# RWKV-7 inside a one-layer decoder trunk: chunk products kept per head in 64x64 blocks, the inverse joined once for all chunks, and chunk groups run offset with one projection k block per step

## The chip, the cores and the metric

The kernel runs on one core of a Trainium2 chip. The metric is the device time of one execution in microseconds (us), the median of several runs. A shorter time is better.

## What is computed

One layer of a hybrid decoder over 1024 tokens of width 1024, in fp32. A projection of the normed input feeds three mixers (HGRN-2, a dilated-window attention, RWKV-7); their outputs go through an output projection, and a gated feed-forward part and a per-layer embedding follow.

```python
z = rmsnorm(h) @ w_in                      # 1024 x 4096
o_a = hgrn2_mix(...); o_b = dilated_window_mix(...); o_c = rwkv7_mix(...)
h = h + concat(o_a, o_b, o_c) @ w_out
h = h + conv_glu_ffn(rmsnorm(h), ...)
h = h + sigmoid(rmsnorm(h) @ w_g) * (p @ w_p)
```

The change is in RWKV-7: four heads of 64, per head a 64x64 state that every token updates.

```python
def step(state, inp):                      # per head
    r_t, w_t, k_t, v_t, kk_t, a_t = inp
    sa = einsum('vk,k->v', state, -kk_t)
    state = state * w_t[None, :] + sa[:, None] * (kk_t * a_t)[None, :] + v_t[:, None] * k_t[None, :]
    return state, einsum('vk,k->v', state, r_t)
# then a group norm per head, a bonus (r k r_k) v, and a gate
```

## The kernel before

**Layout and precision.** Activations lie transposed, 128 rows of channels by 1024 tokens. A product with a weight is done in three matmuls on parts rounded to fp32r (`mm3`, L139, L141, L143: high x high, low x high, high x low). One projection of 128 output channels (tile `dp`, two PSUM banks, two buffers) is eight k blocks of six 128x512 matmuls, 48 in all. Its weight is loaded by SP (L107), rounded by ScalarE (`whi`, L116), and the remainder taken by GpSimd or VectorE (`wlo`, L118). Its result is scaled on VectorE and put through a sigmoid on ScalarE where it needs one (`zst`, L415 to L420), then stored to DRAM (`z`, L410) and loaded again by its user (`zl`, L448).

**RWKV in chunks.** A tile holds a pair of heads, 64 rows each; the head pairs are p = 0 and 1. The 1024 tokens are 16 chunks of 64. `rwkv_prep` makes the decayed operands `ar` (a and r), `bhat` and `khat`, `v` and the bonus (`bon`, L573). `rwkv_scores` (L608) makes all chunks' 64x64 scores in TensorE (`sc`), copied by ScalarE. `rwkv_inverse` inverts 32x32 blocks by substitution on VectorE for all chunks at once (L630, L632), and sends the two diagonal blocks through DRAM into the layout that the loop reads (`Tz`, `Uz` to `Tc`, L641; `T` on SP's queue, `U` on ScalarE's).

**The loop.** `rwkv_main` runs four groups of four chunks, one after the other (`rwkv_group`, L697 to L826). A group copies its operands into block-diagonal 128x128 tiles (`abd`, `bbd`, `kbd`, `addend`; GpSimd and ScalarE), transposes these and `v` (L732, L736), spreads the scores (L748) and the inverse's blocks (L756) over 128x128, joins the two halves of each inverse (`py` L763, `pu` L778, and a predicated copy), and then makes `pk`, `px` (L789), `pgm` (L796), `pn`, the chain of states (`pS`, with `S` on VectorE, L815) and the outputs `pyo`. `by_head` (L595) issues a product per head, 64x64; `px`, `pgm`, `py` and `pu` are 128x128 products on block-diagonal operands, half of them zeros. `rwkv_norm` normalises a half of the tokens and ends with output transposes (`yt`, L682) and the gate product (`pg`, L686).

**What sets the order.** The kernel is written under a tile framework whose scheduler orders every engine's instructions by when their parts were written and by dependences; a tile that takes over another tile's memory waits for that tile's last user. So the projections that the other mixers need (`project_rest`, 22 from a list `js`) serve as filler. `FILL` says how many are written where: six ahead of the first loop, four behind it, four ahead of the second and four behind it. Four go to the next phase. Behind each loop, the second half's `yt` and `pg` are written behind the third of the four projections (`finish` at i == 2), with the fourth after them. The scheduler moves a few matmuls of these projections into the loops and most into the preparation and the substitution.

**What follows.** HGRN and the attention run interleaved, with the four projections left (`zp`) as filler. The attention loads q, k, v of its first two heads on GpSimd's queue (L448), its mask on ScalarE's queue (L339), transposes v (`vt`, L1026) and makes scores (`swq`, L1043). HGRN's first loads are on SP's queue (L448).

Of the kernel before, what the change touches and what calls it, by code (L numbers as in the profile page):

```python
# [10 lines left out]
F32 = mybir.dt.float32  # L11
# [7 lines left out]
P = 128  # L19
# [18 lines left out]
CC_ID, CC_BONE, CC_MSK, CC_Q, CC_HG, CC_RU = 0, 128, 256, 512, 640, 640 + 9 * 128  # L38
NC0 = 640
NCC = CC_RU + 128  # L40


def shape_constants():
# [6 lines left out]
    c[:, CC_MSK:CC_MSK + P] = same & (pp < ff)  # L50
    c[:, CC_MSK + P:CC_MSK + 2 * P] = same & (pp <= ff)
# [5 lines left out]
    c[:, CC_Q:CC_Q + P] = pp // 32 == ff // 32  # L57
    c[:, CC_RU:CC_RU + P] = same & (ff % 64 >= 32) & (pp % 64 < 32)
# [33 lines left out]
class Trunk:  # L92
# [183 lines left out]
    def setup(self):  # L276
# [6 lines left out]
        self.msk = self.cst[:, CC_MSK:CC_MSK + 2 * P]  # L283
        self.qmask = self.cst[:, CC_Q:CC_Q + P]
        self.cmask = cp.tile([P, NCC - NC0], U8, name="cmask")
        self.umask = self.cmask[:, CC_RU - NC0:CC_RU - NC0 + P]
# [109 lines left out]
    def project_rest(self, js):  # L396
# [3 lines left out]
        for j in js:  # L400
            ps = self.proj(j)
# [9 lines left out]
            self.z[j] = d  # L411

# [49 lines left out]
    def rwkv(self):  # L462
# [7 lines left out]
        for p in (0, 1):  # L470
# [16 lines left out]

    def rwkv_prep(self, p, tp, lt, d):
# [57 lines left out]
        ar = self.slots.tile([P, 16, 2, 64], F32, tag="rk_ar", name=self.nm("ar"), bufs=1)  # L546
# [7 lines left out]
        nc.vector.scalar_tensor_tensor(ar[:, :, 0, 1:], kk3[:, :, 1:], -1.0, g3[:, :, :63], ALU.mult, ALU.mult)  # L554
        nc.scalar.activation(ar[:, :, 0, 0:1], kk3[:, :, 0:1], AF.Copy, scale=-1.0)
# [7 lines left out]
        nc.vector.tensor_tensor(ar[:, :, 1, :], c3(r), g3, ALU.mult)  # L563
# [13 lines left out]
    def block_diag(self, pool, name, src, eng):  # L577

        if (pool, name) not in self.bd:
            t = pool.tile([P, 4, 2, 64], F32, tag=name, name=self.nm(name), bufs=1)  # L580
            self.nc.gpsimd.memset(t, 0.0)
            self.bd[(pool, name)] = t
        t = self.bd[(pool, name)]
        for h in (0, 1):
# [27 lines left out]
    def rwkv_inverse(self, p, tp, d):  # L612
# [22 lines left out]
        for nm, t, q in (("T", Tb, nc.sync), ("U", Ub, nc.scalar)):  # L635
# [4 lines left out]
            for o in range(4):  # L640
                q.dma_start(c[32 * o:32 * o + 32], z4[o])  # L641
# [1069 lines left out]
```

## Time and profile before

| what | value |
|---|---|
| median of three runs | 1498.32 us (1496.51 to 1498.58) |
| profiled execution | 1494.42 us, span 1492.6 us |
| TensorE clock granted, mean | 0.994 |
| busy share TensorE, VectorE, ScalarE, GpSimd | 97%, 73%, 42%, 28% |
| first loop, head pair 0 | 150.66 to 213.60 us of the span |
| second loop, head pair 1 | 350.08 to 413.76 us |

A line of the timeline has the start, the duration, engine, source line and operation, the tile written and those read, the matmul's shape and the number of instructions merged; in brackets stands the idle time before it and what ended it. Fp32 matmuls appear as two records for each instruction, so a pair of 64x64 products, one per head, is "x4". PE is TensorE, DVE VectorE, ACT ScalarE, POOL GpSimd, SP SyncE; a q behind an engine's name is its DMA queue. Matmul ends are modelled, so that neighbours overlap; starts are what can be compared.

### The profile page before, as it was taken

To read this page: it belongs to the slowest core of one execution; us is meant where nothing else is said; L and a number is where in the kernel's file an instruction comes from. 1 tells how busy PE (TensorE), PEld (TensorE's weight loads), DVE (VectorE), ACT (ScalarE), POOL (GpSimd) and SP (SyncE) were. 2 spreads that over 40 slices of the span, in tenths; PEclk is the share of its full clock that TensorE was granted. 3 is DMA by queue.
4 is the path that set the end of the run, shared out by engine and by line. 5 is a ranking of instruction groups with operands and counts; after the bars stand their busy time and mean duration, and the time that the engine had idled before them with its cause. 6 is when DMAs were issued, how large, how long until landed. Compare 5 with 4: busy or idle time off the path is not lost.

```text
span 1492.6 us, 21436 instructions
## 1 busy us (share of the span) xinstructions
PE 1446.8 (97%) x8142; PEld 1183.3 (79%) x8142; DVE 1090.7 (73%) x1580; ACT 619.5 (42%) x1072; POOL 420.3 (28%) x346
## 2 busy tenths in 40 slices
PE   7999999999999999999999999999999999999996
PEld 5778878778777787778778888888888888888885
DVE  6586552775556678736878888888888799867685
ACT  6422421413323445424454444444444444455542
POOL 2323311314222132112124444455554000002332
PEclk9999999999999999999999999999999999999998
DMA  5224002023042131164323333333332893352343
GB/s 202 74 64 141 30 30 85 29 92 86 30 176 86 58 119 44 44 253 170 127 100 106 106 106 106 106 106 106 106 101 72 303 316 97 106 165 61 118 146 125
DMA packets 79735, 167.92 MB, mean 112 GB/s; under 512 B 19920, under 2 KB 22096, under 8 KB 79632
## 3 DMA queue, kind: packets, MB, share of 16 engines
q1 hardware_dynamic: 66176, 146.49, 29.3%
q10 hardware_dynamic: 12368, 15.99, 3.1%
q0 software_dynamic: 1088, 4.06, 0.7%
q8 instruction: 64, 1.05, 0.3%
q14 instruction: 39, 0.32, 0.1%
HBM read 120.12 MB, written 46.40 MB: 112 GB/s over the span
## 4 chain that ended last, share of the span: by engine, by line
PE 48%; issue 2%; DVE 1%; POOL 1%; ACT 0%; DMA 0%; POOLq 0%; ACTq 0%; DVEq 0%
PE bg L1198 16%; PE bv L1198 12%; PE bv L1492 7%; PE bg L1492 7%; PE bv L139 1%; PE bv L141 1%; PE bv L143 1%; PE bg L139 1%; PE bg L143 1%; PE bg L141 1%; PE dp L143 1%; PE dp L139 1%; PE dp L141 1%; POOL wlo L118 0%; DVE h L1224 0%
## 5 line engine op out<-in xcount | busy, mean ns | idle before, releaser
L139 PE MATMUL dp<-xh,whi 128*128 128x512 f32 x544 | 186.0, 399 | 9.8 <-ACT xh L381 8.5
L141 PE MATMUL dp<-xl,whi 128*128 128x512 f32 x544 | 185.2, 396 | 0.5 <-DVE xl L382 0.3
L143 PE MATMUL dp<-xh,wlo 128*128 128x512 f32 x544 | 183.0, 394 | 0.3 <-POOL wlo L118 0.3
L118 POOL TENSOR_TENSOR wlo<-raw,whi 128x512 fp32r<-128x512 f32 x84 | 134.3, 1618 | 76.3 <-ACT whi L116 76.3
L118 POOL TENSOR_TENSOR wlo<-wraw,whi 128x512 fp32r<-128x512 f32 x60 | 81.3, 1354 | 248.7 <-ACT whi L116 231.5
L116 ACT CAST whi<-wraw 128x512 fp32r<-128x512 f32 x120 | 73.0, 617 | 172.0 <-PE dp L141 138.1
L1198 PE MATMUL bg<-t,whi 128*128 128x512 f32 x352 | 133.2, 389 | 0.0
L139 PEld LDWEIGHTS dp<-xh,whi 128*128 128x128 f32 x544 | 102.2, 189 | 33.3 <-ACT xh L381 8.5
L141 PEld LDWEIGHTS dp<-xl,whi 128*128 128x128 f32 x544 | 102.5, 189 | 25.6 <-DVE xl L382 2.8
L143 PEld LDWEIGHTS dp<-xh,wlo 128*128 128x128 f32 x544 | 102.2, 189 | 22.6 <-issue 1.0
L118 POOL TENSOR_TENSOR wlo<-s,whi 128x512 fp32r<-128x512 f32 x44 | 64.8, 1472 | 173.8 <-ACT whi L116 173.8
L1492 PE MATMUL bg<-t,whi 128*128 128x512 f32 x308 | 95.2, 390 | 0.0
L1492 PE MATMUL bv<-t,whi 128*128 128x512 f32 x308 | 94.8, 389 | 0.0
L116 ACT CAST whi<-raw 128x512 fp32r<-128x512 f32 x88 | 52.6, 619 | 96.8 <-issue 51.2
L116 ACT CAST whi<-s 128x512 fp32r<-128x512 f32 x66 | 38.9, 620 | 121.3 <-PE bg L1198 113.5
L192 POOL TENSOR_TENSOR rst<-rst,mhalf 128x4 f32<-128x4 f32 (+1 forms) x9 | 10.9, 1217 | 242.5 <-DVE rst L188 225.5
L1198 PEld LDWEIGHTS bg<-t,whi 128*128 128x128 f32 x352 | 66.1, 188 | 13.7
L118 DVE TENSOR_TENSOR wlo<-wraw,whi 128x512 fp32r<-128x512 f32 x60 | 47.0, 785 | 30.7 <-ACT whi L116 26.0
L1492 PEld LDWEIGHTS bv<-t,whi 128*128 128x128 f32 x308 | 57.8, 188 | 12.0
L1492 PEld LDWEIGHTS bg<-t,whi 128*128 128x128 f32 x308 | 57.8, 188 | 11.9
L1198 PE MATMUL bg<-t,wlo 128*128 128x512 f32 x176 | 67.2, 389 | 0.0
L1488 ACT CAST t<-t 128x512 fp32r<-128x512 f32 x77 | 47.8, 622 | 45.9 <-PE bv L1492 32.7
(415 smaller groups left out, 3624.7 us busy)
## 6 DMA issues: line engine op xcount, KB each, us to landing
raw<-in_ffn_up_dram SPq DMA_DIRECT2D x44, 512.0 KB, 3.5
wraw<-in_w_in_dram SPq DMA_DIRECT2D x30, 512.0 KB, 3.3
z<-zst SPq DMA_DIRECT2D x18, 512.0 KB, 2.7
gb<-ct SPq DMA_DIRECT2D x33, 256.0 KB, 2.2
t<-gb SPq DMA_DIRECT2D x33, 256.0 KB, 3.0
t<-gt SPq DMA_DIRECT2D x33, 256.0 KB, 2.7
zl<-z SPq DMA_DIRECT2D x16, 512.0 KB, 3.7
wraw<-in_ple_gate_dram SPq DMA_DIRECT2D x16, 512.0 KB, 3.4
```

What stands on the lines that cost most here:

```text
L116: self.cast = nc.scalar.copy(hi, src).ins
L118: eng.tensor_tensor(lo, src, hi.bitcast(F32), ALU.subtract)
L139: nc.tensor.matmul(ps[hf], wh, xh[hf], start=first, stop=False)
L141: nc.tensor.matmul(ps[hf], wh, xl[hf], start=False, stop=False)
L143: nc.tensor.matmul(ps[hf], wl, xh[hf], start=False, stop=last)
L192: nc.gpsimd.tensor_tensor(r2, r, self.mhalf[:, :n], ALU.pow)
L1198: nc.tensor.matmul(ps, w[part == 2][:, s], X[k][part == 1], start=start and k == part == 0, stop=k == 3 and part == 2, skip_group_check=no ...
L1488: nc.scalar.copy(xh, x)
L1492: nc.tensor.matmul(ps[m], wt[part == 2][:, m * P:(m + 1) * P], (xh, xl)[part == 1], start=k == part == 0, stop=k == NK - 1 and part == 2)
```

## The change

- Operands stay compact, 64 rows for each head. There are no block-diagonal tiles and no spreads; every product in the loop is issued per head, 64 rows by 64 columns, or 128 wide where two operands share weights (`sk`, `px`, `pgm`). Transposes are plain matmuls against a 64x64 identity (`id64`). All work tiles of a group have two buffers.
- The scores are masked as they leave PSUM, on VectorE, four times per head pair (before: a copy on ScalarE).
- The halves of the inverse are joined once for all 16 chunks (`rwkv_join`), in 32x32 products with two copies each on ScalarE, ahead of the groups. U's loads go into one half of a zeroed tile.
- `rwkv_main` runs 22 slots. A group begins every four slots and does a stage per slot (transposes; scores; `pk`; `px`; `pgm` and `pn`; four steps of the chain; outputs), so that two or three groups are under way. Each slot takes one k block (six matmuls) of a projection from a generator. The next projection's weight is loaded at the fourth k block.
- `FILL` is now the projections written ahead of each loop and the total of each head pair: (5, 10) and (4, 8). The second half's normalisation takes six k blocks at each of its steps; in the second pair the fill is at its end there: 32 ahead of the loop, 22 in it, 10 in the normalisation.

```diff
         nc = self.nc
-        for j in js:
-            ps = self.proj(j)
+        w = None
+        for i, j in enumerate(js):
+            w = w or self.load_w(self.a["w_in"][j])
+            ps = self.dps.tile([P, T], F32, tag="dp", name=self.nm("dp"))
+            nxt = None
+            for k in range(ND):
+                self.mm3({0: ps[:, :HT], 1: ps[:, HT:]}, w(k), self.X[k], k == 0, k == ND - 1)
+                if k == 3 and i + 1 < len(js):
+                    nxt = self.load_w(self.a["w_in"][js[i + 1]])
+                if k < ND - 1:
+                    yield
+            w = nxt
             t = self.keep.tile([P, T], F32, tag="zst", name=self.nm("zst"), bufs=2)
             kind = (j - 8) % 4 if j < 24 else 2
             parts = [(t, ps, self.R)]
...
             d = self.zpool.tile([P, T], F32, tag=f"z{j}", name=f"z{j}")
             nc.sync.dma_start(d, t)
             self.z[j] = d
+            yield
...
-            self.project_rest([next(js) for _ in range(self.FILL[2 * p])])
+            lead, n = self.FILL[p]
+            fill = self.project_rest([next(js) for _ in range(n)])
+            for _ in range(8 * lead):
+                next(fill)
             with tc.tile_pool(name=f"rk{p}", bufs=1) as rp:
-                self.rwkv_main(p, rp, sg, d)
-            for i in range(self.FILL[2 * p + 1]):
-                self.project_rest([next(js)])
-                if i == 1:
-                    finish = self.rwkv_norm(p, sg, d, 1)
-                if i == 2:
-                    finish()
+                self.rwkv_main(p, rp, sg, d, fill)
+            self.rwkv_norm(p, sg, d, 1, fill)
+            for _ in fill:
+                pass
         self.rest = list(js)
-    FILL = (6, 4, 4, 4)
+    FILL = (5, 10), (4, 8)
...
             ps = mxp.tile([P, 4, 64], F32, tag="mx", name=self.nm("sc"))
-            for u in range(4):
-                for q, _ in self.QUADS:
-                    nc.tensor.matmul(ps[q, u, :], be3[q, 4 * g + u, :], d["ar"][q, 4 * g + u, 0, :], start=True, stop=True)
-            nc.scalar.copy(sc3[:, cs, :], ps)
+            for u, q in self.UNITS:
+                nc.tensor.matmul(ps[q, u, :], be3[q, 4 * g + u, :], d["ar"][q, 0, 4 * g + u, :], start=True, stop=True)
+            nc.vector.tensor_tensor(sc3[:, cs, :], ps, self.msk[:, 0, :].unsqueeze(1).broadcast_to([P, 4, 64]), ALU.mult)
         d["sc"] = sc3
...
         for nm, t, q in (("T", Tb, nc.sync), ("U", Ub, nc.scalar)):
             z = self.zpool.tile([64, T], F32, tag=f"{nm}z{p}", name=f"{nm}z{p}")
             q.dma_start(z, t.rearrange("p i c -> p (i c)"))
-            c = self.slots.tile([P, 16, 32], F32, tag=f"rk_{nm}", name=self.nm("Tc"), bufs=1)
             z4 = z.rearrange("(o u) (i c) -> o i u c", o=4, c=32)
-            for o in range(4):
-                q.dma_start(c[32 * o:32 * o + 32], z4[o])
-            d[nm] = c
-
-    def rwkv_main(self, p, rp, sg, d):
+            if nm == "T":
+                d["T"] = c = self.slots.tile([P, 16, 32], F32, tag="rk_T", name=self.nm("Tc"), bufs=1)
+                for o in range(4):
+                    q.dma_start(c[32 * o:32 * o + 32], z4[o])
+            else:
+                d["U"] = c = self.slots.tile([P, 16, 2, 32], F32, tag="rk_U", name=self.nm("Uc"), bufs=1)
+                nc.gpsimd.memset(c, 0.0)
+                for o in range(4):
+                    q.dma_start(c[32 * o:32 * o + 32, :, o % 2, :], z4[o])
+
+    def rwkv_main(self, p, rp, sg, d, fill):
         y = self.slot("y")
-        y3 = y.rearrange("p (c v) -> p c v", v=64)
-        S = None
-        d.update(y=y, y3=y3)
-        for g in range(4):
-            S = self.rwkv_group(p, g, rp, d, y3, S)
-            if g == 2:
-                self.rwkv_norm(p, sg, d, 0)()
-
-    def rwkv_norm(self, p, sg, d, hf):
+        d.update(y=y, y3=y.rearrange("p (c v) -> p c v", v=64), S=None)
+        live = [self.rwkv_join(rp, d)]
+        for slot in range(22):
+            if slot % 4 == 0 and slot < 16:
+                live.append(self.rwkv_group(slot // 4, rp, d))
+            if slot == 15:
+                live.append(self.rwkv_norm_steps(p, sg, d, 0))
+            live = [s for s in live if next(s, STOP) is not STOP]
+            next(fill, None)
+
+    def rwkv_join(self, rp, d):
+
+        nc, T1, U = self.nc, d["T"], d["U"]
+        py = self.mxp.tile([P, 16, 32], F32, tag="mx", name=self.nm("py"))
+        for c in range(16):
+            for lo, hi in self.HALVES:
+                nc.tensor.matmul(py[hi, c, :], d["sc"][lo, c, 32:64], T1[lo, c, :], start=True, stop=True)
+        Y = rp.tile([P, 16, 32], F32, name=self.nm("Y"))
+        for _, hi in self.HALVES:
+            nc.scalar.copy(Y[hi], py[hi])
+        yield
+        pu = self.mxp.tile([P, 16, 32], F32, tag="mx", name=self.nm("pu"))
+        for c in range(16):
+            for lo, hi in self.HALVES:
+                nc.tensor.matmul(pu[lo, c, :], Y[hi, c, :], U[hi, c, 1, :], start=True, stop=True)
+        for lo, _ in self.HALVES:
+            nc.scalar.copy(U[lo, :, 1, :], pu[lo])
+        d["U64"] = U.rearrange("p c b i -> p c (b i)")
+        yield
+
+    HALVES = tuple((slice(a, a + 32), slice(a + 32, a + 64)) for a in (0, 64))
+
+    def rwkv_norm(self, p, sg, d, hf, fill):
+        for _ in self.rwkv_norm_steps(p, sg, d, hf):
+            for _ in range(6):
+                next(fill, None)
+
+    def rwkv_norm_steps(self, p, sg, d, hf):
...
         nc.vector.tensor_tensor(y3, y3, rs.unsqueeze(2).broadcast_to([P, 8, 64]), ALU.mult)
+        yield
+        yield
+        pt = mxp.tile([P, HT], F32, tag="mx", name=self.nm("yt"))
+        for c in range(8):
+            for q in self.QUADS:
+                nc.tensor.matmul(pt[q, c * 64:(c + 1) * 64], y3[q, c, :], self.id64[q], start=True, stop=True)
...
+    def rwkv_group(self, g, rp, d):
         nc, mxp = self.nc, self.mxp
         cs = slice(4 * g, 4 * g + 4)
+        ar, gC = d["ar"], d["gC"]
         def c3(t):
             return t.rearrange("p (c i) -> p c i", i=64)[:, cs, :]
+        def rt(name, shape, bufs=2):
             return rp.tile(shape, F32, tag=name, name=self.nm(name), bufs=bufs)
+        def mx(name, *shape):
+            return mxp.tile([P, *shape], F32, tag="mx", name=self.nm(name))
+
+        def wide(t, *dims):
+            return t.unsqueeze(1).broadcast_to([P, 4, *dims])
+
+        a, r = ar[:, 0, cs, :], ar[:, 1, cs, :]
+        be, kh, v = c3(d["be"]), c3(d["kh"]), c3(d["v"])
+        W, KV = rt("W", [P, 2, 4, 128]), rt("KV", [P, 2, 4, 64])
+        for srcs, dst in (((a, be), W[:, :, :, 0:64]), ((kh, v), KV)):
+            pt = mx("pt", 2, 4, 64)
+            for i, src in enumerate(srcs):
+                for u, q in self.UNITS:
+                    nc.tensor.matmul(pt[q, i, u, :], src[q, u, :], self.id64[q], start=True, stop=True)
             nc.scalar.copy(dst, pt)
+        yield
+        AR = rt("AR", [P, 4, 2, 64])
+        ps = mx("sk", 4, 2, 64)
+        for u, q in self.UNITS:
+            nc.tensor.matmul(ps[q, u, :, :], kh[q, u, :], ar[q, :, 4 * g + u, :], start=True, stop=True)
+        nc.vector.tensor_tensor(AR, ps, wide(self.msk, 2, 64), ALU.mult)
+        ps = mx("sr", 4, 64)
+        for u, q in self.UNITS:
+            nc.tensor.matmul(ps[q, u, :], be[q, u, :], r[q, u, :], start=True, stop=True)
+        nc.vector.tensor_tensor(W[:, 1, :, 64:128], ps, wide(self.msk[:, 1, :], 64), ALU.mult)
+        yield
+        pk = mx("pk", 4, 64)
+        for u, q in self.UNITS:
+            nc.tensor.matmul(pk[q, u, :], AR[q, u, 0, :], KV[q, 1, u, :], start=True, stop=True)
+        nc.scalar.copy(W[:, 0, :, 64:128], pk)
+        yield
+        X = rt("X", [P, 4, 128])
+        px = mx("px", 4, 128)
+        for u, q in self.UNITS:
+            nc.tensor.matmul(px[q, u, :], d["U64"][q, 4 * g + u, :], W[q, 0, u, :], start=True, stop=True)
+        nc.scalar.copy(X, px)
+        yield
+        MG = rt("MG", [P, 4, 128])
+        pg = mx("pgm", 4, 128)
+        for u, q in self.UNITS:
+            nc.tensor.matmul(pg[q, u, :], X[q, u, 0:64], W[q, 1, u, :], start=True, stop=True)
+        nc.vector.tensor_tensor(MG[:, :, 0:64], pg[:, :, 0:64], wide(self.id64, 64), ALU.add)
+        nc.vector.tensor_tensor(MG[:, :, 64:128], pg[:, :, 64:128], r, ALU.add)
+        N = rt("N", [P, 4, 64])
+        pn = mx("pn", 4, 64)
+        for i in range(0, 8, 2):
+            for u, q in self.UNITS[i:i + 2]:
+                nc.tensor.matmul(pn[q, u, :], W[q, 1, u, 0:64], X[q, u, 64:128], start=True, stop=False)
+            for u, q in self.UNITS[i:i + 2]:
+                nc.tensor.matmul(pn[q, u, :], KV[q, 0, u, :], KV[q, 1, u, :], start=False, stop=True)
+        nc.vector.tensor_tensor(N, pn, gC[:, cs].unsqueeze(2).broadcast_to([P, 4, 64]), ALU.mult)
+        yield
+        before = []
         for u in range(4):
+            t = 4 * g + u
+            S = d["S"]
+            before.append(S)
+            if t < 15:
+                d["S"] = rt("S", [P, 64], bufs=7)
+                if S is None:
+                    nc.vector.tensor_copy(d["S"], N[:, u, :])
+                else:
+                    pS = mx("pS", 64)
+                    for q in self.QUADS:
+                        nc.tensor.matmul(pS[q], MG[q, u, 0:64], S[q], start=True, stop=True)
+                    nc.vector.scalar_tensor_tensor(d["S"], pS, gC[:, t:t + 1], N[:, u, :], ALU.mult, ALU.add)
+            yield
+        py = mx("pyo", 4, 64)
...
```

In the first loop, TensorE's order before the change: the end of one group's stages. Here `dp` is the projection, `pS` the chain's product and `pyo` the output.

```order
L595 MATMUL pyo_1513<-vt_1398,RKt_1426 64x64 x2
L141 MATMUL dp_1940<-xl_94,whi_1932 128x512
L595 MATMUL pS_1526<-S_1514,GM_1485 64x64 x2
L595 MATMUL pyo_1513<-S_1514,GM_1485 64x64 x2
L595 MATMUL pyo_1513<-X_1476,rb_1396 64x64 x2
L595 MATMUL pyo_1513<-vt_1398,RKt_1426 64x64 x2
L143 MATMUL dp_1940<-xh_109,wlo_1934 128x512
L595 MATMUL pS_1537<-S_1525,GM_1485 64x64 x2
```

The same loop after the change, a slot and the beginning of the next two (`pS` is of the group before, `pk` and `px` of this one):

```order
L141 MATMUL dp_1222<-xl_116,whi_1109 128x512
L141 MATMUL dp_1222<-xl_100,whi_1109 128x512
L143 MATMUL dp_1222<-xh_115,wlo_1111 128x512
L143 MATMUL dp_1222<-xh_99,wlo_1111 128x512
L801 MATMUL pS_1439<-S_1409,MG_1334 64x64 x2
L765 MATMUL pk_1443<-KV_1366,AR_1411 64x64 x8
L139 MATMUL dp_1222<-xh_117,whi_1109 128x512
L139 MATMUL dp_1222<-xh_101,whi_1109 128x512
L141 MATMUL dp_1222<-xl_118,whi_1109 128x512
L141 MATMUL dp_1222<-xl_102,whi_1109 128x512
L143 MATMUL dp_1222<-xh_117,wlo_1111 128x512
L143 MATMUL dp_1222<-xh_101,wlo_1111 128x512
```

Single projection matmuls between the steps of the chain have become blocks of six, one block in each slot, with a step of the chain and a stage of the next group between two blocks.

Behind the second loop, TensorE's order before the change (`yt` and `pg` end the second pair's normalisation; `dp_3834` is one more projection of 48 matmuls, of which the first two are shown):

```order
L143 MATMUL dp_3759<-xh_119,wlo_3757 128x512
L143 MATMUL dp_3759<-xh_103,wlo_3757 128x512
L682 MATMUL yt_3814<-cst,y_2879 128x128 x4
L686 MATMUL pg_3821<-sg_445,par 128x512
L139 MATMUL dp_3834<-xh_105,whi_3826 128x512
L139 MATMUL dp_3834<-xh_89,whi_3826 128x512
```

And after it, to the first filler of the next phase (`zp`):

```order
L143 MATMUL dp_3836<-xh_119,wlo_3766 128x512
L143 MATMUL dp_3836<-xh_103,wlo_3766 128x512
L710 MATMUL yt_3889<-cst,y_2902 64x64 x16
L714 MATMUL pg_3908<-sg_445,par 128x512
L1034 MATMUL swq_3954<-zl_3932,zl_3930 128x128
L1034 MATMUL swq_3955<-zl_3932,zl_3930 128x128
L1034 MATMUL swq_4026<-zl_3932,zl_3930 128x256
L1017 MATMUL vt_3941<-cst,zl_3934 128x128 x4
L1017 MATMUL vt_3947<-cst,zl_3934 128x128 x4
L139 MATMUL zp_3982<-xh_105,whi_3972 128x512
```

No projection is left behind `pg`: the attention's scores and its transposes of v stand next, on tiles `zl` that GpSimd's queue loads.

GpSimd's order at the same place, before (`gnr` belongs to the second half's normalisation):

```order
L722 COPY addend_2892<-ar_2397 64x4x64 x2
L448 DMA zl_3906<-z_2131 128x1024
L448 DMA zl_3908<-z_2204 128x1024
L448 DMA zl_3910<-z_2674 128x1024
L676 TENSOR_TENSOR gnr_3746<-gnv_3743,mhalf 128x8
```

And after:

```order
L702 TENSOR_TENSOR gnr_3815<-gnv_3812,mhalf 128x8
L118 TENSOR_TENSOR wlo_4391<-wraw_4383,whi_4389 128x512
L458 DMA zl_3930<-z_2141 128x1024
L458 DMA zl_3932<-z_2216 128x1024
L458 DMA zl_3934<-z_2697 128x1024
L857 MEMSET hS_4009 128x512
```

The three loads stood behind the last group's copies and ahead of the normalisation's `gnr`; now they stand behind it and behind a weight's remainder.

More of the change, by code (lines that the diff above doesn't have):

```diff
@@ new lines, in rwkv_group @@
+        py = mx("pyo", 4, 64)
+        for i in range(0, 8, 2):
+            two = self.UNITS[i:i + 2]
+            for u, q in two:
+                nc.tensor.matmul(py[q, u, :], W[q, 1, u, 64:128], X[q, u, 64:128], start=True, stop=False)
+            for u, q in two:
+                nc.tensor.matmul(py[q, u, :], AR[q, u, 1, :], KV[q, 1, u, :], start=False, stop=before[u] is None)
+            for u, q in two:
+                if before[u] is not None:
+                    nc.tensor.matmul(py[q, u, :], MG[q, u, 64:128], before[u][q], start=False, stop=True)
@@ L827, in hgrn_setup @@
+        nc.scalar.copy(d["y3"][:, cs, :], py)
+        yield
     def hgrn_setup(self):
```

175 lines of the change are left out of this document (24 added, 151 removed).

## The prediction

> **What bounds the kernel now.** I read the page's busy shares and chain first, then the two RWKV loops in windows, then the TensorE timeline inside one group.
>
> ```profile
> PE 1446.8 (97%) x8142; PEld 1183.3 (79%) x8142; DVE 1090.7 (73%) x1580; ACT 619.5 (42%) x1072; POOL 420.3 (28%) x346
> PE 48%; issue 2%; DVE 1%; POOL 1%; ACT 0%; DMA 0%; POOLq 0%; ACTq 0%; DVEq 0%
> ```
>
> TensorE is busy 97% of the span and no other engine ends more than 1% of the chain. So an edit pays by what it takes off TensorE, and costs by every hole it opens there.
>
> ```profile
> 150.66:213.60 62.94, 62.00 (x788) 50.46 (x786) 33.59 (x62) 25.56 (x67) 16.53 (x24) 1.00 0.05 18
> 350.08:413.76 63.68, 62.53 (x789) 50.86 (x787) 36.94 (x66) 25.64 (x68) 19.76 (x30) 1.00 0.10 35
> ```
>
> These are the loops of the two head pairs (first transpose to last `pyo`; columns: length, then PE, PEld, DVE, ACT, POOL busy with counts, clock, DMA share, GB/s). TensorE has almost no hole in either. Projection matmuls (`dp`) lie in them as filler, 33 and 34 by the order.
>
> ```profile
> 788.11 5.44 PE bg L1198 x24
> ```
>
> A 128x512 matmul in a dense stretch of the chain takes 5.44/24 = 0.227 us, so filler is 7.5 and 7.7 us and the loops' **own** time is 55.5 and 56.0. Filler only moves. One group, the second of the first pair:
>
> ```profile
> 166.38 0.66 PE L732 MATMUL pt<-cst,abd 128*128 128x128 f32 x4
> 168.32 1.13 PE L763 MATMUL py<-T,ABt 128*128 128x128 f32 x8 [0.20 <-ACT xr L733]
> 169.90 1.04 PE L773 MATMUL sc<-ar,khat 64*64 64x128 f32 x16
> 170.87 1.16 PE L778 MATMUL pu<-U,Y 128*128 128x128 f32 x8
> 173.60 1.46 PE L789 MATMUL px<-xr,U 128*128 128x192 f32 x8
> 175.04 1.99 PE L796 MATMUL pgm<-rb,X 128*128 128x256 f32 x8
> 176.96 0.33 PE L595 MATMUL pn<-X,rb 64*64 64x64 f32 x4
> 177.24 0.28 PE L595 MATMUL pn<-X,rb 64*64 64x64 f32 x4
> 177.94 0.28 PE L595 MATMUL pS<-S,GM 64*64 64x64 f32 x4
> 178.53 0.28 PE L595 MATMUL pyo<-vt,RKt 64*64 64x64 f32 x4
> 178.74 0.49 PE L141 MATMUL dp<-xl,whi 128*128 128x512 f32 x1
> 179.16 0.33 PE L595 MATMUL pS<-S,GM 64*64 64x64 f32 x4
> ```
>
> Ends are modelled, so I price by starts. A pair of 64x64 products (both heads, x4 records): from 177.24 to 177.94 are six, 0.117 us each. The 64x128 pairs: 0.97/4 = 0.243. `py` 1.06, `pu` 1.09, `px` 1.44, `pgm` 1.92. One `dp` between 64-row products: 178.53 to 179.16 is 0.63; less a pair and a matmul, 0.29 is lost per visit.
>
> **The loops.** After, each head pair has 285 pair-equivalents of 64x64: transposes 64, `sk` 32, `sr` 16, `pk` 16, `px` 32, `pgm` 32, `pn` 32, `pS` 14, `pyo` 47. That is 33.2, and 0.5 more for the 48 wide pairs (0.243 against 2 x 0.117): 33.7. The first half's output transposes and gate product, inside the loop as before: 8 pairs and two passes of 128x512, 1.4. Switches: 22 slots, a visit each, 22 x 0.29 = 6.4, 7 where a slot has a second. A stage that follows another form starts 0.05 late (176.96 to 177.24 is 0.28 for two pairs): some 30, 1.5. The join: 32 pairs of 32x32 products; no row shows one. If a record costs what it does at 64 wide, 3.7; if half, 1.9; no reason makes it cheaper still. I take the middle, 2.8. Waits: each stage's result is now needed one slot on, under six `dp` (1.36 us), and its copy of 0.4 to 0.8 us (rows below) fits unless it stands behind another, so I allow 1 (0 to 4). Sum 33.7 + 1.4 + 6.7 + 1.5 + 2.8 + 1.0 = 47.1. **Gain 8.4 and 8.9, together 17.3 (11 to 21).** The second halves' output transposes, outside the loops, go from four records at 0.11 to 8 pairs: 2 x 0.5 = **+1.0**.
>
> Beside the join's price: the Trainium skill, TensorE: Matmul & The Clock Gate, part 1, states that starts of matmuls never come closer than about 25 ns however small they are; by it the 128 records are an estimated 3.2 and the sum 0.4 later.
>
> What goes from the other engines (the block-diagonal copies, the spreads of `AB`, `T` and `U`, the predicated copy) was hidden: of all of it only `py`'s 0.20 shows on TensorE, and it is counted at nothing. With each projection move its weight load, casts and `z` store; the load of the next block now leaves at the fourth k block, four slots ahead of its use (a slot is (47.1 + 126 x 0.227)/22 = 3.4 us, so some 14 us), and is counted at nothing too; if it were late, TensorE would wait for it there.
>
> **The stages ahead of the loops.**
>
> ```profile
> 81.42 2.08 PE L608 MATMUL sc<-ar,bhat 64*64 64x64 f32 x64 [1.45 <-DVE ar L554]
> 88.32 1.96 PE L573 MATMUL bon<-prod,cst 128*128 128x512 f32 x4 [0.97 <-DVE prod L569]
> 291.73 2.08 PE L608 MATMUL sc<-ar,bhat 64*64 64x64 f32 x64 [1.44 <-DVE ar L554]
> 298.76 3.08 PE L573 MATMUL bon<-prod,cst 128*128 128x512 f32 x4 [2.24 <-DVE prod L569]
> 298.00:300.00 2.00, 1.24 (x3) 0.56 (x4) 2.00 (x4) 0.00 (x0) 0.43 (x2) 0.86 0.40 62
> 300.00:302.00 2.00, 2.00 (x4) 0.94 (x3) 1.13 (x3) 0.00 (x0) 0.00 (x0) 0.50 0.20 36
> 302.00:304.00 2.00, 2.00 (x8) 1.59 (x7) 1.17 (x2) 0.00 (x0) 0.00 (x0) 0.78 0.99 295
> L802 DVE TENSOR_TENSOR N<-pn,gC 128x256 f32<-128x256 f32 x4 | 1.7, 424 | 1.6 <-PE pn L595 1.6
> ```
>
> The order puts 60 `dp` before the first pair's `sc` instead of 53: 7 x 0.227 covers the 1.45. The score masks go to VectorE, ahead of `prod`: four of 128x256, nearest row 0.42, 1.7; the order also puts 23 `dp` instead of 16 behind `sc`, 1.6, so that hole stays. **-1.5.** In the second pair `sc` has 49 before it as before, and behind it 23 for 11, 2.7, against 1.7 and the `v` step now ahead of `prod`: **-0.3** (+1 to -2). The last windows show what a hole of 2.24 costs besides: the granted clock falls to 0.86, 0.50 and 0.78, (0.14 + 0.50 + 0.22) x 2 = 1.7 us. The holes of 1.45 left it at full.
>
> The Trainium skill, TensorE: Matmul & The Clock Gate, part 1, has the clock halved after an idle window of about 3.4 us; here 2.24 sufficed. By its figure the hole of the next part, 2 to 4, would cost 1.7 less.
>
> **The join's operands.** The old loop met the inverse first on VectorE (`T` at 349.83); the new one meets it on TensorE, in `py`, and everything queued on TensorE waits behind it.
>
> ```profile
> 344.48 2.21 SPq L641 DMA_DIRECT2D Tc<-Tz  x4
> 349.83 0.69 DVE L756 TENSOR_TENSOR T<-Tc,cst 128x512 f32<-128x512 f32 x1 [0.71 <-DMA Tc<-Uz]
> 350.08 0.60 PE L732 MATMUL pt<-cst,abd 128*128 128x128 f32 x4
> ```
>
> In the second pair 201 `dp` lie between `sc` and `py` instead of 222: 21 x 0.227 = 4.8, so TensorE is there at 58.35 - 4.8 = 53.6 after `sc` starts. The four loads are out by 346.7 and read at 349.83, so they land 55 to 58 after `sc`. Hole 2 to 4, with the clock 1.7 more where it passes 2: **+4.5** (0 to 6). In the first pair the loads come earlier and TensorE just behind them: 0.
>
> **Behind the second loop.** This is the large loss I see.
>
> ```profile
> 414.63 1.72 POOL L448 DMA_DIRECT2D zl<-z  x3 [20.04 <-PE pyo L595]
> 431.95 0.60 PE L682 MATMUL yt<-cst,y 128*128 128x128 f32 x4
> 432.84 1.03 PE L139 MATMUL dp<-xh,whi 128*128 128x512 f32 x2
> 433.29 0.80 DVE L683 TENSOR_SCALAR oc<-yt,par 128x512 f32<-128x512 f32 x1
> 433.41 1.03 ACT L418 ACTIVATE zst<-dp 128x1024 f32<-128x1024 f32 x1 [1.10 <-DVE dp L323]
> 434.61 1.22 DVE L420 TENSOR_TENSOR zst<-zst,dp 128x1024 f32<-128x1024 f32 x1
> 435.74 0.68 DVE L684 TENSOR_TENSOR oc<-oc,bv 128x512 f32<-128x512 f32 x1
> 436.49 2.38 SPq L448 DMA_DIRECT2D zl<-z  x4
> 441.91 0.81 DVE L857 TENSOR_SCALAR zl<-zl,olb,lb 128x1024 f32<-128x1024 f32 x1 [2.12 <-DMA zl<-z]
> 444.14 1.03 PE L1026 MATMUL vt<-cst,zl 128*128 128x128 f32 x8
> 414.63:424.00 9.37, 9.37 (x43) 7.73 (x42) 5.35 (x9) 3.36 (x6) 4.67 (x5) 1.00 0.66 230
> 436.40:446.00 9.60, 9.60 (x47) 7.85 (x46) 5.45 (x9) 3.01 (x6) 1.66 (x2) 1.00 0.86 312
> ```
>
> Before, the attention's three loads (512 KB each, GpSimd's queue) leave at 414.63, when the loop's operand tiles come free, with 29 us in hand; HGRN's four leave on SP at 436.49, behind `oc`, under a last projection from 432.84 to 444.14. Now all fill is spent before the last `yt`: TensorE runs `yt`, the gate product, and next `swq`, which reads GpSimd's loads. These now lie over tiles that live to the end of the normalisation, so GpSimd's three, SP's four, the mask on ACT's queue and the last `z` store start together, about 3 us after the last `dp` (`zst` 1.2, `oc` 0.8 and 0.7). That is 9 x 0.52 = 4.7 MB. At the 312 GB/s of the last row all are in after 15.1, and the first four, if they go ahead, after 6.7; the two that `swq` needs are the first on their queue, so I take 9, nearer the lower end. TensorE then resumes 12 after the last `dp`, of which the output transposes and the gate product cover 1.4, and the clock takes 1.7: 3 + 9 - 1.4 + 1.7 = **+12** (10 to 23). Behind this place the order on all engines is as before and TensorE nearly dense, so the loss stays.
>
> The Trainium skill, DMA: Bandwidth & Descriptors, section on queues, rings and completion order, has each DMA engine take turns between the queues' rows; by it GpSimd's two loads (1.05 MB) get a third, later half, of 312 GB/s, an estimated 8.4 instead of 9, and the term would be 11.7.
>
> **Sum.** -17.3 + 1.0 - 1.5 - 0.3 + 4.5 + 12 = -1.6. The profiled execution took 1494.42 (span 1492.6 and 1.8 around it), 3.9 under the median of the runs, 1498.32: 1492.8 there, **1496.7 by the median**. A difference under 0.2%, 3.0 us, can't be told from none.
>
> **Rivals.**
> *The holes stay small.* GpSimd's two loads come with the first four transfers, after 6.7, and `py` finds its loads landed. Then the last term is 10 and the join's 0: 6.5 less, **1490**. For it: the two are the first of their queue, and the first pair's join comes out without a hole. Against: nine transfers start, not four.
> *The transfers share evenly (slower).* Place: `swq` after the last gate product. If all nine progress alike, the two land with the last, at 15.1 instead of 9, or at 20 by the 230 GB/s of the window from 414.63: +6 to +11, **1505**. It decides once they land more than 13.6 after their release. For it: HGRN's load of 436.49 was read only 5.4 later, among four. Against: transfers are issued about 0.6 apart, so that the early ones are ahead.
> *The slots wait.* Six `dp` cover 1.36, but a sigmoid of 1.0 or a `zst` of 1.2 (both rows above) may stand before the copy on ACT or VectorE. At 0.25 more for each of 44 slots: +11, **1507**. For it: in one stretch of the old loop `py` already waited 0.20 for ACT. Against: both engines are half idle there.
>
> **Chances.** Forecast 0.42 (own range 1490 to 1502: 0.24 within 0.2%, 0.14 faster, 0.04 slower); small holes 0.22 (0.21 faster, 0.01 same); even sharing 0.22 (slower); waiting slots 0.14 (0.11 slower, 0.02 same, 0.01 faster). Faster 0.36, same 0.27, slower 0.37. The range takes in the small holes with a fuller loop gain, 1487, and the waiting slots, 1507.
>
> **What would show it.** Loops of own time near 47 with holes under 0.3 a slot; `py` of the second pair idle 2 to 4 on a DMA; `swq` after the last gate product idle 8 to 13 on GpSimd's loads with the clock at 0.5 behind it; no hole before the first `sc`. I am wrong if that `swq` waits under 5 us, or if TensorE idles in most slots.

## The result and the profile after

The changed kernel takes 1500.38 us (median of 17 runs, 1497.76 to 1501.87), the kernel before 1495.35 (17 runs, 1492.37 to 1498.95): a ratio of 1.0029 with an interval of 1.0021 to 1.0038. It is slower by 0.3%, some 5 us. The prediction said 1.6 faster, so the sign was wrong, though the time lies in its range.

The busy shares and the chain of waits of the profiled execution after (span 1499.5, before 1492.6):

```profile
PE 1444.2 (96%) x8910; PEld 1168.8 (78%) x8910; DVE 1062.3 (71%) x1556; ACT 593.2 (40%) x976; POOL 379.8 (25%) x276
PE 48%; issue 2%; DVE 1%; POOL 1%; ACT 0%; DMA 0%; POOLq 0%; ACTq 0%; DVEq 0%
```

TensorE is still what bounds the kernel, and its busy time fell by only 2.6 us. The two loops (first join product to last `pyo`) in windows, columns as in the prediction:

```profile
141.47:214.82 73.35, 73.35 (x1237) 59.32 (x1236) 24.71 (x55) 17.68 (x34) 6.37 (x5) 1.00 0.13 45
333.58:405.72 72.14, 72.14 (x1226) 57.80 (x1226) 24.37 (x53) 18.89 (x35) 6.74 (x5) 1.00 0.17 52
```

They are longer than before (62.94 and 63.68), but by the order 126 and 116 projection matmuls stand in them instead of 33 and 34. Less 0.2267 for each, the own time is 44.8 and 45.8, where it was 55.5 and 56.0: 10.7 and 10.1 less. TensorE is busy throughout.

To see where this gain goes, I compare the start of the same matmul in both traces, each less 0.2267 for every projection matmul that the order has ahead of it. The difference, after minus before, is the change's lead (negative: ahead).

| place | before | after | lead | forecast lead |
|---|---|---|---|---|
| first loop begins | 150.66 - 528 x 0.2267 | 141.47 - 480 x 0.2267 | +1.7 | -1.5 |
| first loop ends | 213.60 - 561 x 0.2267 | 214.82 - 606 x 0.2267 | -9.0 | -9.9 |
| second loop begins | 350.08 - 1087 x 0.2267 | 333.58 - 1066 x 0.2267 | -11.7 | -5.2 |
| second loop ends | 413.76 - 1121 x 0.2267 | 405.72 - 1182 x 0.2267 | -21.9 | -14.1 |
| first `zp`, all projections done | 445.52 | 440.00 | -5.5 | -1.6 |
| a feed-forward matmul (`bv` on `tp6h`) | 776.75 | 772.82 | -3.9 | -1.6 |
| end of the span | 1492.6 | 1499.5 | +6.9 | -1.6 |

Two losses stand out: 16 us between the second loop and the first `zp`, and 11 us from the feed-forward part to the end, whose code the change doesn't touch at all.

**The first loss** is the place that the prediction named. The timeline after, the loads and TensorE:

```profile
421.00 1.15 PE L710 MATMUL yt<-cst,y 64*64 64x64 f32 x32
422.08 1.12 PE L714 MATMUL pg<-sg,par 128*128 128x512 f32 x2
423.84 2.76 SPq L458 DMA_DIRECT2D zl<-z  x4
424.32 1.73 POOL L458 DMA_DIRECT2D zl<-z  x3 [1.70 <-DVE oc L712]
436.08 0.80 PE L1034 MATMUL swq<-zl,zl 64*128 64x128 f32 x4 [12.88 <-DMA zl<-z]
438.38 1.97 PE L1017 MATMUL vt<-cst,zl 128*128 128x128 f32 x8
```

and windows over it:

```profile
426.00:428.00 2.00, 0.00 (x0) 0.00 (x0) 0.00 (x0) 0.00 (x0) 0.58 (x2) 0.73 1.02 379
428.00:430.00 2.00, 0.00 (x0) 0.00 (x0) 0.00 (x0) 0.00 (x0) 0.00 (x0) 0.50 1.02 418
442.00:444.00 2.00, 2.00 (x7) 1.52 (x6) 1.97 (x4) 0.00 (x0) 0.00 (x0) 0.50 0.71 256
444.00:446.00 2.00, 2.00 (x10) 1.65 (x9) 0.21 (x1) 0.00 (x0) 0.00 (x0) 1.00 0.00 0
```

Seven loads leave from 424 on, the DMA engines are full at some 418 GB/s (the last two columns), and the first `swq` runs at 436. From issue to landing the transfers took (the last number is the median in us):

```profile
zl<-z SPq DMA_DIRECT2D x4, 512.0 KB, 10.3
zl<-z POOLq DMA_DIRECT2D x3, 512.0 KB, 10.7
```

GpSimd's three land at 433.17, 435.73 and 438.26; `swq` needs the first two. The granted clock (third from the end) is 0.50 from 427 on, and stays there for 8 us after TensorE resumes.

**The second loss** shows only when the groups of matmuls are put side by side. Feed-forward, second part, where every matmul reads a tile `t` (mean ns of one is the second number behind the bar); before:

```profile
L1492 PE MATMUL bg<-t,whi 128*128 128x512 f32 x308 | 95.2, 390 | 0.0
L1492 PE MATMUL bv<-t,whi 128*128 128x512 f32 x308 | 94.8, 389 | 0.0
```

and after:

```profile
L1483 PE MATMUL bg<-t,whi 128*128 128x512 f32 x308 | 97.2, 396 | 0.0
L1483 PE MATMUL bv<-t,whi 128*128 128x512 f32 x308 | 96.9, 395 | 0.0
```

The same code, the same shape, the same full clock, no idle time in either, and each matmul takes 6 ns longer (starts 0.2331 apart instead of 0.2268).

### The profile page after: what moved, and what is told of

The parts are those of the page before. It is cut to its first block, busy times and chain, and to the rows that moved or that the text cites. A ratio compares the mean times of both kernels' runs of the same rounds, so it can differ in the third digit from the quotient of the medians.

```text
span 1499.5 us, 22728 instructions
## 1 busy us (share of the span) xinstructions
PE 1444.2 (96%) x8910; PEld 1168.8 (78%) x8910; DVE 1062.3 (71%) x1556; ACT 593.2 (40%) x976; POOL 379.8 (25%) x276
## 4 chain that ended last, share of the span: by engine, by line
PE 48%; issue 2%; DVE 1%; POOL 1%; ACT 0%; DMA 0%; POOLq 0%; ACTq 0%; DVEq 0%
PE bg L1189 15%; PE bv L1189 12%; PE bv L1483 7%; PE bg L1483 7%; PE bv L139 1%; PE bv L141 1%; PE bv L143 1%; PE dp L143 1%; PE dp L141 1%; PE dp L139 1%; PE bg L139 1%; PE bg L141 1%; PE bg L143 1%; POOL wlo L118 0%; POOL rst L192 0%
## 5 line engine op out<-in xcount | busy, mean ns | idle before, releaser
L1189 PE MATMUL bg<-t,whi 128*128 128x512 f32 x352 | 135.4, 395 | 0.0
L1483 PE MATMUL bg<-t,whi 128*128 128x512 f32 x308 | 97.2, 396 | 0.0
L192 POOL TENSOR_TENSOR rst<-rst,mhalf 128x4 f32<-128x4 f32 (+1 forms) x9 | 10.3, 1148 | 249.2 <-DVE rst L188 231.6
```

The costliest lines, as they stand in the source:

```text
L192: nc.gpsimd.tensor_tensor(r2, r, self.mhalf[:, :n], ALU.pow)
L1189: nc.tensor.matmul(ps, w[part == 2][:, s], X[k][part == 1], start=start and k == part == 0, stop=k == 3 and part == 2, skip_group_check=no ...
L1483: nc.tensor.matmul(ps[m], wt[part == 2][:, m * P:(m + 1) * P], (xh, xl)[part == 1], start=k == part == 0, stop=k == NK - 1 and part == 2)
```

## The experiments

**Theories for the second loss.** By the compiled programs' addresses, one thing differs in the feed-forward part. The change shrinks two constants below the weight tiles, `cst` from 640 to 448 columns and `cmask` from 1280 to 1152 bytes. So the weight tiles (`whi`, `wlo`) lie 896 bytes lower in each partition, 128 mod 256, while the tiles `t` at the other end stayed. Before, the moving operand and the weights of all 128x512 matmuls but 12 have the same address mod 256; after, 1740 with fp32r operands differ by 128. The theory: that difference costs 6.4 ns a matmul, 1740 x 6.4 ns = 11.1 us. The rival: something else in the program (weights' timing, DMA traffic) slows them.

*Addresses as before.* Padding a small constant by 896 bytes puts every weight tile back:

```diff
-        self.omm = cp.tile([P, 8], F32, name="omm")
+        self.omm = cp.tile([P, 232], F32, name="omm")[:, :8]
```

> The changed kernel with 896 unused bytes per partition in the constants' pool, so that all tiles behind it lie where they lay before the change. Address theory: a 128x512 matmul whose moving operand and weights differ by 128 modulo 256 in their byte addresses starts its successor about 6.4 ns later; the change made 1740 such pairs (none before), 11 us, nearly all in the feed-forward part. Then this run takes 1489 +- 2 us, the feed-forward groups are back at 389 ns mean from 395, and the start-to-start step there at 0.2268 us. Rival, the drift comes from the chip (clock, heat, another device) or from the RWKV part in another way: 1500 us and 395 ns as in the changed kernel.

Measured: 1491.13 us (9 runs), ratio to the kernel before 0.9966 (0.9953 to 0.9978); 9.3 under the changed kernel and just above the 1487 to 1491 expected. The same groups:

```profile
L1483 PE MATMUL bg<-t,whi 128*128 128x512 f32 x308 | 95.1, 390 | 0.0
L1483 PE MATMUL bv<-t,whi 128*128 128x512 f32 x308 | 94.8, 389 | 0.0
```

*A pad that keeps the difference.* The same line with `[P, 72]`, 256 bytes more:

> The same with 256 unused bytes: every address behind the constants moves, but none of the differences modulo 256 does. Address theory: 1500 +- 2 us and 395 ns, as the changed kernel. Rival, that any other layout or the larger pool does it: 1489 us.

Measured: 1500.68 us (9 runs), ratio 1.0030 (1.0018 to 1.0042), and the slow groups again:

```profile
L1483 PE MATMUL bg<-t,whi 128*128 128x512 f32 x308 | 97.3, 396 | 0.0
L1483 PE MATMUL bv<-t,whi 128*128 128x512 f32 x308 | 96.9, 395 | 0.0
```

So it isn't a pad or a move of the tiles as such: 256 bytes do nothing, 896 take the loss away. The theory held for a difference of 128.

*A difference of 64.* The same line with `[P, 24]`:

> The changed kernel with 64 unused bytes: pairs that differed by 128 modulo 256 in their addresses now differ by 64, the others by 0. If only a difference of 128 costs, the feed-forward groups are at 389 ns and the run at 1490; if any difference modulo 256 costs the same, 395 ns and 1500; if the conflict has a finer grain, something between.

Measured: 1498.68 us in one run, only 1.7 under the changed kernel. The groups on `t`, whose addresses now differ by 64, lie between:

```profile
L1483 PE MATMUL bv<-t,whi 128*128 128x512 f32 x308 | 95.7, 392 | 0.0
L1483 PE MATMUL bg<-t,whi 128*128 128x512 f32 x308 | 95.7, 391 | 0.0
```

But groups that keep a common address, 388 and 389 in the changed kernel, became slower:

```profile
L1189 PE MATMUL bg<-tp5l,whi 128*128 128x512 f32 x84 | 33.3, 396 | 0.0
L1189 PE MATMUL bv<-tp7h,whi 128*128 128x512 f32 x84 | 33.2, 395 | 0.0
```

So the groups on `t` keep between a quarter and a half of their loss, and part of what they gain is lost again in pairs for which the theory has no cost. The difference mod 256 isn't the whole rule; what else counts stays open.

**Theories for the first loss.** `swq` waits for GpSimd's loads, and these leave late. Either they wait for too much (the attention's pool is handed over as a whole), or too little work is left to cover them, or, as the prediction's rival had it, their own transfer sharing with six others is what counts.

*Each tile waits for its own predecessor only*, in the changed kernel:

```diff
-        with tc.tile_pool(name="hg", bufs=1) as slots, tc.tile_pool(name="sw", bufs=1) as sp:
+        with self.pool("hg") as slots, self.pool("sw") as sp:
```

> The changed kernel in which the pools of the next phase wait for each tile's own last user instead of for everything in the pools that lay there; order of all engines unchanged. Theory: the hole of 12.9 us at the attention's first scores exists because GpSimd's loads wait for the last normalisation; they then leave about 4.7 us earlier and without SP's four loads beside them, the hole shrinks to 3 to 5, the clock stays at 1.00 or falls for one window, and the run takes 1490 +- 3 us. Rival, the transfers' rate alone sets it (all nine still move 4.7 MB): hole 9 or more, 1497 to 1500 us.

Measured: 1501.65 us (6 runs), ratio 1.0037 (1.0024 to 1.0050), no gain.

```profile
421.88 1.27 POOL L118 TENSOR_TENSOR wlo<-wraw,whi 128x512 fp32r<-128x512 f32 x1 [9.96 <-ACT whi L116]
423.09 1.73 POOL L458 DMA_DIRECT2D zl<-z  x3
434.98 0.80 PE L1034 MATMUL swq<-zl,zl 64*128 64x128 f32 x4 [11.25 <-DMA zl<-z]
```

The loads leave only 1.2 earlier, and the first `swq` runs 11.9 after that. My theory, that with a wait for each tile alone they would leave 4.7 earlier, failed in this form. The lines show why: GpSimd's order is as it was, and in it the loads stand behind the `wlo` of a later weight, which ends at 423.15. So the run doesn't tell what a wait for each tile would give in another order. The rival, that the transfers' rate sets the hole, fits the 11.25.

*Fill kept behind the normalisation*, in the changed kernel: the second pair's last norm takes two k blocks a step instead of six, so that six k blocks stand behind `pg`.

```diff
-            for _ in range(6):
+            for _ in range(2 if p else 6):
```

> The changed kernel with two k blocks instead of six at each step of the second pair's normalisation, so that six k blocks (36 matmuls, 8.2 us) come behind the gate product. Theory: they cover all but about 3 to 5 us of the hole and the clock mostly holds: 1490 +- 3 us. Rival, the loads are held by something behind the filler (the last projection's store, the clock): the hole only moves, 1498 to 1500 us.

Measured: 1496.58 us (11 runs), ratio 1.0004 (0.9993 to 1.0015): 3.8 less than the changed kernel, where more was expected.

```profile
417.80 2.06 SPq L458 DMA_DIRECT2D zl<-z  x4
418.36 1.73 POOL L458 DMA_DIRECT2D zl<-z  x3 [6.26 <-PE dp L141]
426.00:428.00 2.00, 0.00 (x0) 0.00 (x0) 1.24 (x1) 0.53 (x2) 1.38 (x2) 0.63 1.01 412
432.63 1.94 PE L1017 MATMUL vt<-cst,zl 128*128 128x128 f32 x8 [8.70 <-DMA zl<-z]
```

The loads leave 6 earlier, but `vt` needs the last of them, and starts 14.3 after the first has left; 8.7 stay open, and the clock still falls (0.63 on the mean of the window shown, 0.50 behind it).

*Addresses as before, with more fill*: the pad, a ninth projection for the second pair taken from the next phase, and four k blocks a step.

```diff
-    FILL = (5, 10), (4, 8)
+    FILL = (5, 10), (4, 9)
...
-            for _ in range(6):
+            for _ in range(4 if p else 6):
```

> E1 (896 unused bytes) and a ninth projection in the second pair, taken from the four of the next phase, with four k blocks at each normalisation step: ten k blocks (60 matmuls, 13.6 us) come behind the gate product. Theory: the hole of 12.9 us and the clock's 4 behind it come from nine transfers that start together and land together about 13 us later, so filler of that length closes it: holes of at most 3 us there, clock at 1.00, and 1491.1 - 12.9 - 4 + 3 = 1477 us, up to 1483 if the next phase misses its filler. Rival, the next phase needs that filler as much: holes of 8 or more at its products, 1487 to 1491.

Measured: 1487.77 us (5 runs), ratio 0.9945 (0.9929 to 0.9962), 3.4 under the pad alone. `vt` starts with an idle time of 0.36, so that the hole is closed. But the next phase has one projection less:

```profile
531.89 2.05 PE L890 MATMUL hsc<-qt,ks 128*128 128x128 f32 x8 [5.19 <-DVE qt L895]
```

From 500 to 560 TensorE is busy for 52.87, against 58.67 with the pad alone. Most of what the tail gained is given back there: fill is moved, not made, as the rival said.

*Addresses as before, and the mask out of the way.* In the compiled program of the changed kernel the RWKV slots end at byte 185280 of a partition (the loop's tiles begin there), and the attention's pool begins at 183232: they overlap by 2048 bytes, under the pool's first tile, the attention's mask. Before, the pool began at 184128, just where the slots ended, so that it had only the loop's tiles to wait for. A pool handed over as a whole makes the loads wait for the last users of the slots, `oc` and `pg`. With the mask in HGRN's pool that overlap is gone:

```diff
-            self.swmask = sp.tile([P, T], F32, name="swmask")
+            self.swmask = slots.tile([P, T], F32, name="swmask")
```

> E1 with the attention's mask (4096 bytes per partition) taken from HGRN's pool instead of being the first tile of the attention's pool. The attention's pool then begins where the RWKV slots end, no longer 4096 bytes inside them, and its three loads need only the last group's outputs. Theory: the hole came from that overlap; the loads leave at about 405 instead of 424, land before the gate product, TensorE goes on with transposes and scores and meets only HGRN's loads later: the hole of 12.8 falls to 5 or less, most of the clock's 4 comes back, 1476 to 1481 us. Rival, the shared rate of the transfers holds TensorE at the next product as well (HGRN's four loads, the mask and the store still start together): holes of 9 or more in total there, 1486 to 1491.

Measured: 1480.80 us (5 runs), ratio 0.9901 (0.9885 to 0.9916), 10.3 under the pad alone.

```profile
406.46 1.73 POOL L458 DMA_DIRECT2D zl<-z  x3 [1.61 <-PE pyo L813]
410.02 1.66 POOL L702 TENSOR_TENSOR gnr<-gnv,mhalf 128x8 f32<-128x8 f32 x1 [1.84 <-PE dp L141]
423.31 1.04 PE L1017 MATMUL vt<-cst,zl 128*128 128x128 f32 x8
431.98 0.29 DVE L1041 CUSTOM_DVE_ANT_0 lg<-swq,swmask 128x128 f32<-128x128 f32 x1 [7.15 <-DMA swmask<-in_swm_dram]
432.34 0.70 PE L1034 MATMUL swq<-zl,zl 64*128 64x256 f32 x2 [1.90 <-DVE sden L1041]
434.12 3.40 PE L869 MATMUL hsc<-zl,hk 128*128 128x128 f32 x16 [1.08 <-ACT lg L1043]
```

The loads leave at 406.46 behind the last `pyo`, as they did before the change, 18 earlier than in the changed kernel, and `vt` and `swq` follow `pg` without a wait. Of 12.9 there remain 3.0; the 1.90 of them ends with VectorE, which waits 7.15 for the mask's own load there. This is the main cause of the first loss: less the missing fill than 2 KB of overlap. The overlap works for the most part through the order: without it the scheduler puts the loads ahead of `gnr` again, while the wait alone cost little where the order stayed (1.2, by the run with a wait for each tile). The smaller constants shift the slots and the pool alike; it is the slots that grew, by 2048 bytes, the second half of the columns of `U`.

*The same with two k blocks a step*, both edits above together:

> E8 with E4's six k blocks (8.2 us) behind the gate product. Theory: these cover what is left of HGRN's loads, holes there under 2 us, 1474 to 1478 us, some 3 below E8. Rival, nothing is left to cover after E8, or the rest sits behind VectorE's own chain: within 1.5 us of E8.

Measured: 1477.37 us (4 runs), ratio 0.9882 (0.9867 to 0.9898). This version beats both kernels: 1.2% under the kernel before. What is left there is one hole:

```profile
428.15 0.79 PE L1034 MATMUL swq<-zl,zl 64*128 64x128 f32 x2 [3.15 <-DVE zst L425]
```

**The masks on VectorE.** The pad, and the scores copied by ScalarE without their mask, as the kernel before had it. The mask can go because nothing later reads what it sets to zero:

```diff
-            nc.vector.tensor_tensor(sc3[:, cs, :], ps, self.msk[:, 0, :].unsqueeze(1).broadcast_to([P, 4, 64]), ALU.mult)
+            nc.scalar.copy(sc3[:, cs, :], ps)
```

> E1 with the scores copied by ScalarE again instead of masked by VectorE (the mask changes no value that is read). The scheduler then puts 16 and 11 projection matmuls between scores and bonus again, not 23 and 23. Theory: the mask's side effect on the order is what closed the second pair's hole of 2.24 us and saved its clock loss of 1.7, and let the inverse start earlier: that hole and a wait of 2 to 4 at the join come back, +3 to +6 us over E1 (1494 to 1497). Rival, the masks only burden VectorE: holes in both preparations shrink by 1.6 and the run takes 1488 to 1490.

Measured: 1489.84 us (5 runs), ratio 0.9953 (0.9935 to 0.9970), about the pad alone (0.9966, 0.9953 to 0.9978).

```profile
290.81 3.10 PE L583 MATMUL bon<-prod,cst 128*128 128x512 f32 x4 [2.22 <-DVE prod L579]
```

The hole ahead of the second pair's `bon`, which the change had removed, is back although VectorE has less to do, and the clock from 280 to 300 is 0.91 on the mean. The theory's other half failed: `py` doesn't wait, and the run isn't 3 to 6 slower. In the first pair the hole ahead of `bon` shrinks from 1.63 to 0.82, as the rival had it there. The copies change the order around these places; what the masks cost by themselves stays open, and it is too small to see in the time.

## Why the prediction was wrong

**The failed step** is "Behind this place the order on all engines is as before and TensorE nearly dense, so the loss stays". The order was as before, the durations weren't: 1740 matmuls of 6.4 ns more, 11 us from 772 to the end. I compared orders and counts and took the price of a 128x512 matmul as fixed; I never asked what the smaller constants do to the addresses of tiles that the change doesn't name. Without that term the lead at the feed-forward matmul of the table, -3.9, would have stayed; the padded kernel shows it, 5.1 under the kernel before. That -3.9 is near the -1.6 of the sum is luck in part: the terms ahead of it were off by +3.2 (first preparation), -3.5 (loops), -7.5 (between them) and +5.5 (behind them), and these nearly cancel.

**The loops**: right in mechanism, low in size. The gain was 20.8 instead of 17.3, at the end of the 11 to 21 given.

```profile
163.69 0.33 PE L801 MATMUL pS<-S,MG 64*64 64x64 f32 x4
163.85 0.63 PE L765 MATMUL pk<-KV,AR 64*64 64x64 f32 x16
164.41 0.73 PE L139 MATMUL dp<-xh,whi 128*128 128x512 f32 x2
166.00 0.33 PE L801 MATMUL pS<-S,MG 64*64 64x64 f32 x4
```

From `pS` at 163.69 to the next at 166.00 is 2.31. Less five pairs (0.117 each) and six projection matmuls (1.36), 0.37 is left for the switches, close to the 0.29 and two late starts of 0.05 that I had put. What was too dear is the waits: the loops have none, where I allowed 1, so the waiting slots as a rival fall.

The other is the join, which is two of these (64 records from 141.47 to 142.60, 1.13):

```profile
141.47 1.20 PE L659 MATMUL py<-Tc,sc 32*32 32x32 f32 x64
142.60 0.39 PE L750 MATMUL pt<-cst,ar 64*64 64x64 f32 x6
```

That is 2.3 for a head pair, against 2.8. With both, 47.1 becomes 45.6, beside the 44.8 and 45.8 measured. The Trainium skill, TensorE: Matmul & The Clock Gate, part 1, has starts of matmuls no closer than about 25 ns; 1.13 over 64 records is 17.7 ns, so that the measurement doesn't agree here.

**The first pair's preparation**: wrong in sign, +1.7 instead of -1.5. The forecast let the seven more projection matmuls cover `sc`'s wait for a fixed `ar`:

```profile
83.96 2.08 PE L600 MATMUL sc<-ar,bhat 64*64 64x64 f32 x64 [1.23 <-DVE ar L564]
93.10 1.96 PE L583 MATMUL bon<-prod,cst 128*128 128x512 f32 x4 [1.61 <-DVE prod L579]
```

VectorE comes to `ar` 2.5 later than before, though, at 82.61 (1.20 each time):

```profile
80.08 1.20 DVE L554 SCALAR_TENSOR_TENSOR ar<-kkn,gam 128x1008 f32<-128x1008 f32 x1
```

So `sc` starts 2.5 later, 1.6 of it covered, and 1.23 of the 1.45 stay; `bon`'s hole grows from 0.97 to 1.61. What delays VectorE there was not tried; the delay is there already when the reciprocal `ig` starts, at 70.09 instead of 67.05.

**Between the loops**: 2.8 gained (lead -9.0 to -11.7), where I had 4.7 lost. `bon` of the second pair waits no more, which takes the 2.24 and the 1.7 of low clock away, and the join's operands come in time:

```profile
333.58 0.24 PE L659 MATMUL py<-Tc,sc 32*32 32x32 f32 x2 [0.44 <-DMA Tc<-Tz]
```

0.44, not 2 to 4. I had moved TensorE towards a fixed inverse, but the inverse moved as well. VectorE's timeline before

```profile
310.61 1.23 DVE L415 TENSOR_TENSOR zst<-dp,rstd 128x1024 f32<-128x1024 f32 x1 [7.44 <-PE dp L143]
312.35 0.18 DVE L630 TENSOR_TENSOR Tt<-At,Tb 64x31 f32<-64x31 f32 x1
```

and after

```profile
298.27 1.23 DVE L425 TENSOR_TENSOR zst<-dp,rstd 128x1024 f32<-128x1024 f32 x1 [4.76 <-PE dp L143]
299.42 0.17 DVE L622 TENSOR_TENSOR Tt<-At,Tb 64x31 f32<-64x31 f32 x1
```

show a projection's `zst` ahead of it that waits for its projection, 7.4 before and 4.8 after. The inverse starts 15.9 behind `sc` (283.50) instead of 20.6 (291.73).

**Behind the second loop**: named rightly, sized low. +16.4 by the lead and 1.6 more up to the feed-forward part, instead of +12; the hole is 12.9 instead of 10.6, and after it half clock lasts 8 us, some 4 lost instead of 1.7. The two loads that `swq` needs landed 11.4 after the first of them had left: later than the 9 that I took and the 8.4 by turns, but before the 13.6 from which the slower rival, even sharing, decides, and one more of GpSimd's and two of SP's came behind them. So none of the three was right, although the rate came to 418 GB/s instead of 312: the transfers landed nearly in the order of their issue, whatever their queue, so that a weight, the `z` store, the mask and two of HGRN's loads came before the second of these two. That the loads are late because a pool overlaps the slots stood in the prediction as a fact of the order ("now lie over tiles that live to the end of the normalisation"), and there I could have asked whether it was needed; with the pad, moving one tile takes 10 us off.

## What to carry to other kernels

When an edit changes the size of any tile, compare the addresses of all tiles and not only the order: a hot matmul's two operands can lose their common address mod 256, and two pools can come to overlap, in places that the diff doesn't mention. In a profile, put the mean duration of each untouched group beside that of the kernel before; a few ns on a group of 300 is a loss that no wait shows. Fill that is spent early uncovers the loads behind it, but ask first why these loads start late.

## What the runs showed of the hardware

- A 128x512 matmul with fp32r operands took some 6.4 ns more (0.2331 from start to start instead of 0.2268) where the addresses of moving operand and weights in the partition differ by 128 mod 256. With a pad of 64 the same groups took 2 to 3 ns more, but some with a common address 6 to 8 more (388 to 396, 389 to 395). What makes it was not tried.
- The granted clock fell to 0.50 in the hole of 12.9 some 3.7 after the last matmul (423.2 to 426.9 by the mean of 0.73), and came back only 8 after work resumed at 436.1. With the fill behind the normalisation it fell some 2.6 after the last matmul. In the version with the mask moved, holes of 1.90 and 1.08 close together sufficed: 0.70 in

```profile
432.00:436.00 4.00, 2.58 (x11) 2.21 (x12) 3.71 (x9) 1.55 (x5) 0.00 (x0) 0.70 0.07 30
```

- Seven loads of 512 KB and their neighbours, issued within 4 us on three queues, ran at 416 to 418 GB/s together and landed from 431.24 to 438.57 in the order of their issue, but for one pair 0.6 apart. In the run with the fill behind the normalisation the eight (seven and the mask) landed from 423.69 to 432.28 exactly in that order. So what was issued earlier on another queue came first too.
